# Spreading 1/rms over the partitions with the identity, and giving out the square-sum products later

## The chip, the core and the metric

The kernel runs on one core of a Trainium2 chip. Its five engines work side by side, each on its own queue: TensorE (PE in the profile, with its weight loads as PEld), VectorE (DVE), ScalarE (ACT), GpSimd (POOL) and SyncE (SP). The metric is the device time of one execution in microseconds (us); lower is better.

## The reference, cut to what matters

Two decoder layers run over 2048 prompt tokens and 8 sample tokens, 1024 channels wide. Every stage starts with a norm over the channels of a token:

```
def rms_norm(x, g):
    y = x * rsqrt(mean(x * x, axis=-1) + EPS)
    return y * g
...
x = x + mixer(rms_norm(x, norm_mix[l]))             # l = 0: conv branch (layer norm) and DeltaNet, l = 1: pooling
x = x + cross_attention(rms_norm(x, norm_xattn[l]))
...
y = rms_norm(x, norm_final)
```

The layer norm of the conv branch subtracts the mean over 512 channels first and divides by the root of the mean square in the same way.

## The kernel before, in words

Activations lie with channels on the 128 partitions and tokens along the free axis, so a sum over channels is a product on PE. All large products run as three products of a high and a low part (`mm3_steps`). The stages, by their times in the profile:

- `phase1`, to about 1137 us: the memory keys and values, then the input projection over five tiles of tokens (`DT`: three of 512, two of 260). The task `squares` (line 731) sums squares, the task `norms` (line 751) multiplies the roots in, and `dense_start` (line 791) gives PE its main work. The DeltaNet scan overlaps its end.
- `e2`, about 1137 to 1390 us: eight groups of 256 tokens (the first has 264, with the sample's 8). `norm` (line 1537) makes the layer norm of the conv branch.
- `attn` for layer 0, to about 1780 us, and again for layer 1, from about 2440 us to the end. `prep` (line 1640) makes the per-token roots, which go into the softmax's scale; `final` (line 1764) makes the last norm of layer 1.
- `odd_u` (line 1806), to about 2010 us, and `odd_g` (line 1958), to about 2440 us: the pooling mixer. Both multiply spread roots into what leaves PE; `odd_g` takes the roots that `odd_u` has stored in `rr`.
- `sample_attn` (line 2257) runs beside `attn` and `odd_g`: it streams keys and values through three buffers (`a_big`) and multiplies and sums them on DVE.

A norm has three steps. `square_sum` (line 1485) squares on ACT and adds on POOL into `w_sqa`. `token_rstd` (line 423) multiplies `w_sqa` by 64 columns of ones into `ps_ss`, one product per 128 tokens, so that each token's sum stands on its partition; twelve small DVE instructions make the root `rstd` (`rsqrt`, line 410). `spread` (line 437) brings the roots back along the free axis, the same on all partitions: DVE multiplies the identity by each column of roots into a diagonal matrix (`dg`, or the tile `w_sqq` by way of `tok_spread`, line 1512), and PE multiplies that by ones into `ps_bc`, one product over all tokens of the group. There are 37 such calls: 5 in `norms`, 8 each in `e2`, `odd_u`, `odd_g` and `final`. An f32 product is recorded as two passes, each with a weight load of 128 columns.

The order of each engine's queue is fixed when the program is written, by a planner (`Flow`). It keeps a clock for each engine with costs of its own. The main products are a generator; after each few of them `pump` (line 342) looks through the side tasks (`norms`, `prep` and so on). A task gives out instructions up to its next `yield`; `F.cur` is then the planner's time at which its last result is seen, and the task goes on when the planner's clock of PE has reached that (`_step`, line 332, puts `cur` into `item[1]`). A task that yields without having given out anything goes on at once. So a product of a norm stands in PE's queue where the planner believed its operand to be ready; if the operand is later than that, PE waits, since it takes its products in this order.

Of the kernel before, what the change touches and what calls it, by code (L numbers as in the profile page):

```python
# [7 lines left out]
F32 = mybir.dt.float32  # L8
# [397 lines left out]
NMORE = 2  # L406
XGAP, XSTART = 1000.0, 8


def rsqrt(F, pool, y, x, n, tag, eng="dve"):  # L410

# [22 lines left out]
    return r  # L434


def spread(F, C, pool, ppool, r, n, tag, dg=None):

    ncn = (n + 127) // 128
    if dg is None:  # L440
        dg = pool.tile([128, ncn * 128], F32, tag=tag + "dg", name="dg")
    for c in range(ncn):
        F.ts(dg[:, c * 128:(c + 1) * 128], C.ident, r[:, c:c + 1], ALU.mult)
    yield
    ps = getattr(ppool, "bgp", ppool).tile([128, 512], F32, tag="bg", name="ps_bc")
    F.mm(ps[:, 0:n], C.ones, dg[:, 0:n])
    return ps


def ceil128(n):  # L450
    return (n + 127) // 128 * 128
# [200 lines left out]
def phase1(F, C, I, D, st, P, R, mmp, bgp, loaders, mix, hp):  # L652
# [38 lines left out]
    with F.tile_pool(name="x1", bufs=1, side="right") as xp:  # L691
# [59 lines left out]
        def norms():  # L751
            for t, (o, n) in enumerate(DT):
                yield lambda: t in sums and (t < 4 or "kv" in sums)
                dg = xp.tile([128, 512], F32, tag="dg", name="dg", bufs=1)
                bc = yield from spread(F, C, xp, bgp, sums[t], n, "n", dg)
                for k in range(8):
                    x, _ = xs.pop((t, k))
                    F.stt(x, x, C.g_mix[:, 0, k:k + 1], bc[:, 0:n], ALU.mult, ALU.mult)
                    if k == 7:
                        F.now()  # L760
                    yield
                    F.copy(hs(t, 0, k), x)
                    yield
                    F.tt(hs(t, 1, k), x, hs(t, 0, k).bitcast(F32), ALU.subtract, eng=F.ve(n))
                    hfree.give()
                yield
                hdone.add(t)
# [742 lines left out]


def tok_spread(F, C, W, r, n):
    return spread(F, C, W.p, W, r, n, "w", dg=W.t("sqq", [128, ceil128(n)]))


def mm3(F, R, W, name, j, x, n):
# [4 lines left out]
    yield from mm3_steps(F, ps[:, 0:n], 8, (lambda k: w[0][:, k, :], lambda k: w[1][:, k, :]),  # L1521
                         (lambda k: x[0][:, k, :], lambda k: x[1][:, k, :]))
    return ps


SLACK = 1000


def e2(F, C, W, I, D, st, R, bdone, over, grow, spawn):

    ready = {}
    cv, sv = (x.rearrange("b p t -> p b t") for x in (D.c, D.sg))
    xv = I["xT"].rearrange("(k p) t -> p k t", p=128)

    ln, used = {}, set()

    def norm():

        for g in range(NG):
            n = gn(g)  # L1540
            yield lambda: g < 2 or g - 2 in used
            c = W.t("cd"[g % 2], [128, 4, n])
            load_cols(F, c, cv, g)
            yield
            cs = W.t("sqa", [128, n])
            F.red(cs, kt(c), ALU.add)
            yield
            ps = W.bgp.tile([128, 512], F32, tag="bg", name="ps_mean")
            F.mm(ps[:, 0:n], C.ones, cs)
            F.stt(c, ps[:, 0:n].unsqueeze(1).to_broadcast([128, 4, n]), -1.0 / 512, c, ALU.mult, ALU.add)  # L1550
            yield
            acc = square_sum(F, W, c, n)
            yield
            r = tok_rstd(F, C, W, acc, n, 1.0 / 512)
            yield
            ps = yield from tok_spread(F, C, W, r, n)
            F.tt(c, c, ps[:, 0:n].unsqueeze(1).to_broadcast([128, 4, n]), ALU.mult)
            yield
            for q in range(4):
                F.act(c[:, q, :], c[:, q, :], AF.Silu, scale=C.lng[:, q:q + 1], bias=C.lnb[:, q:q + 1])  # L1560
            ln[g] = c

    def prep():
        for g in range(NG):
            n = gn(g)
            sg = W.t("f", [128, 4, n])
            load_cols(F, sg, sv, g)
            yield lambda: g in ln
            c = ln.pop(g)
            F.tt(c, c, sg, ALU.mult)  # L1570
            yield lambda: bdone >= {2 * g, 2 * g + 1}
            b = W.t("f", [128, 4, n])
            F.dma(b, D.b[g])
            tb = F.cur
            F.now()
            res = W.xbuf if g % 2 == 0 else W.mbuf
            yield lambda: W.p2 is not None and res.ok()
            res.take()
            m = W.pair("x" if g % 2 == 0 else "m", n)
            yield from split_steps(F, m[0][:, 0:4], m[1][:, 0:4], c)  # L1580
            used.add(g)
            yield lambda: F.t["pe"] >= tb
            yield from split_steps(F, m[0][:, 4:8], m[1][:, 4:8], b)
            ready[g] = m, res

    def load_x(g, h):
        xr = W.t(f"y{h}", [128, 4, gn(g)])
        load_cols(F, xr, xv[:, 4 * h:4 * h + 4], g)
        return xr

    def dense():
        xr = {(0, h): load_x(0, h) for h in range(2)}
        grown = False

        def wait(cond):
            nonlocal grown
            yield from F.until(lambda: cond() or not grown and over())
            if not grown and over():
                grow()
                grown = True  # L1600
                yield from F.until(cond)

        for g in range(NG):
            n = gn(g)
            yield from wait(lambda: g in ready)
            m, res = ready.pop(g)
            for j in range(8):
                yield from wait(lambda: R.has("wo_e", j))
                ps = yield from mm3(F, R, W, "wo_e", j, m, n)
                if j == 7:  # L1610
                    res.give()
                h, q = j // 4, j % 4
                x = xr[g, h]
                F.tt(x[:, q, :], ps[:, 0:n], x[:, q, :], ALU.add)
                if q == 3:
                    F.dma(D.x1[g][:, 4 * h:4 * h + 4, :], x)
                    if g == 0:
                        F.copy(st.xs[:, 4 * h:4 * h + 4, :], x[:, :, 256:264])
                    if g + 1 < NG:
                        xr[g + 1, h] = load_x(g + 1, h)  # L1620
                if g == NG - 1:
                    R.free("wo_e", j)
                F.now()
            st.done.add(("x", 0, g))
            if g == 0:
                yield from wait(lambda: grown)
                spawn()

    F.spawn(norm(), 1)
    return prep(), dense()  # L1630


def attn(F, C, W, D, st, R, l, xin, xout):
# [6 lines left out]
    def prep():  # L1640
        for g in range(NG):
            acc, ch = None, []
            yield lambda: ("x", l, g) in st.done
            for h in range(2):
                x = W.t("f", [128, 4, 256])
                F.dma(x, xin[g][:, 4 * h:4 * h + 4, 0:256])
                yield
                if h == 0:
                    res = W.xbuf if g == 0 else W.mbuf
                    yield res.ok  # L1650
                    res.take()
                    xs = W.pair("x" if g == 0 else "m", 256)
                    yield W.sq.ok
                    W.sq.take()
                acc = square_sum(F, W, x, 256, acc, h == 1)
                yield from split_steps(F, xs[0][:, 4 * h:4 * h + 4], xs[1][:, 4 * h:4 * h + 4], x)
            yield
            r = tok_rstd(F, C, W, acc, 256, 1.0 / 1024)
            W.sq.give()
            r16 = W.t("r16", [128, 2], 2)  # L1660
            F.ts(r16, r, 1.0 / 16, ALU.mult)
            ready[g] = xs, r16
# [101 lines left out]
    def final(g, y):  # L1764
        yield W.sq.ok
        W.sq.take()
        acc = None
        for h in range(2):
            acc = square_sum(F, W, y[h], 256, acc, h == 1, "pool" if g < NG - 1 else "dve")
        yield  # L1770
        r = tok_rstd(F, C, W, acc, 256, 1.0 / 1024)
        yield
        ps = yield from tok_spread(F, C, W, r, 256)
        W.sq.give()
        for j in range(8):
            h, q = j // 4, j % 4
            F.stt(y[h][:, q, :], y[h][:, q, :], C.g_fin[:, j:j + 1], ps[:, 0:256], ALU.mult, ALU.mult)
            if q % 2:
                F.dma(D.o_y[g][:, j - 1:j + 1], y[h][:, q - 1:q + 1, :])
        if g + 2 < NG:  # L1780
            ys[g + 1] = load_y(g + 1)
        ydone.add(g)
# [23 lines left out]
def odd_u(F, C, W, I, D, st, R, rr):  # L1806
# [5 lines left out]
    def prep():  # L1812
        for g in range(NG):
# [4 lines left out]
            for h in range(2):  # L1818
# [7 lines left out]
                    xs = W.pair("x" if g % 2 == 0 else "m", n)  # L1826
                yield from split_steps(F, xs[0][:, 4 * h:4 * h + 4], xs[1][:, 4 * h:4 * h + 4], x)
            ready[g] = xs, res
            yield
            r = tok_rstd(F, C, W, acc, n, 1.0 / 1024)  # L1830
            F.vcopy(rr[:, g, 0:r.shape[1]], r)
            yield
            ps = yield from tok_spread(F, C, W, r, n)
            if g == 0:
                W.rb = W.t("rb", [128, 2, 264])
# [834 lines left out]
```

## Time and profile before

| | us |
|---|---|
| median of three runs (2884.25 to 2889.04) | 2886.37 |
| the profiled execution | 2889.38 |
| its span, first to last instruction | 2887.7 |
| PE busy (94% of the span), 20202 products | 2721.9 |
| PEld busy (86%) | 2494.4 |
| DVE busy (67%) | 1948.4 |
| ACT busy (35%) | 1012.6 |
| POOL busy (22%) | 647.4 |

Busy times are added per engine; engines overlap. What stands in brackets behind an instruction is the engine's idle time just before it and what ended that. A group "x8" is eight instructions in a row, with its first start and the time to its last end; the ends of products on PE are modelled, so distances between starts are the safer measure.

### The profile page before, as it was taken

What the parts mean: (1) busy time and instruction counts of PE and PEld (TensorE: products, weight loads), DVE (VectorE), ACT (ScalarE), POOL (GpSimd) and SP (SyncE); (2) the same over time, 40 slices, a digit from 0 to 9 for tenths busy, and PEclk for the clock granted to TensorE, in tenths of its full rate; (3) what the DMA queues carried; (4) which work ended last, traced back from release to release, by engine and by line L of the source; (5) the groups of instructions that cost most, each with busy time, mean ns of one, the idle gap of its engine ahead of it and who ended that gap; (6) DMA issues with size and microseconds to landing.
All of it is one profiled execution on the core that took longest, in us unless ns stands there. A gap on an engine that the chain in (4) does not pass through costs nothing.

```text
span 2887.7 us, 52194 instructions
## 1 busy us (share of the span) xinstructions
PE 2721.9 (94%) x20202; PEld 2494.4 (86%) x20202; DVE 1948.4 (67%) x4438; ACT 1012.6 (35%) x2388; POOL 647.4 (22%) x928
## 2 busy tenths in 40 slices
PE   7999999999999888799999999899999998999998
PEld 6878888888888777699888989899999998788987
DVE  6838999989678787776755556867655446665453
ACT  5632133233266454432322235444421113332321
POOL 3301112111053544123222320111012112221210
PEclk9999999999999998899999999899999999999999
DMA  7611122223355666565645434321535556421111
GB/s 240 213 50 41 45 71 56 61 74 115 118 148 160 200 205 189 184 214 190 205 154 165 151 106 145 105 74 67 185 129 169 178 169 201 135 76 67 67 60 51
DMA packets 260297, 377.85 MB, mean 131 GB/s; under 512 B 47440, under 2 KB 155728, under 8 KB 260048
## 3 DMA queue, kind: packets, MB, share of 16 engines
q1 hardware_dynamic: 181328, 267.13, 29.3%
q0 software_dynamic: 20864, 67.39, 7.5%
q10 hardware_dynamic: 57856, 39.99, 4.4%
q8 instruction: 159, 2.61, 0.4%
q14 instruction: 90, 0.74, 0.1%
HBM read 276.38 MB, written 96.40 MB: 129 GB/s over the span
## 4 chain that ended last, share of the span: by engine, by line
PE 51%; DVE 22%; DMA 11%; issue 4%; ACT 3%; POOL 1%; SPq 1%; DVEq 0%; ACTq 0%; POOLq 0%
PE ps_mm L168 44%; DVE cacc L225 7%; PE ps_bg L168 4%; DVE qacc L225 3%; DMA a_big<-d_sq 2%; DMA rraw<-d_VW 1%; DVE a_big L225 1%; DMA w_f<-d_x 1%; DMA a_big<-d_sp 1%; DVE rlo L219 1%; PE ps_pt L172 1%; PE ps_row L168 1%; DMA rraw<-d_G 1%; PE ps_bg L172 1%; POOL w_sqb L219 1%
## 5 line engine op out<-in xcount | busy, mean ns | idle before, releaser
L225 DVE SCALAR_TENSOR_TENSOR cacc<-glu,dww,cacc 128x1024 f32<-128x1024 f32 x240 | 325.0, 1367 | 5.9 <-ACT cacc L186 1.4
L219 POOL TENSOR_TENSOR rlo<-rraw,rhi 128x512 fp32r<-128x512 f32 x132 | 197.3, 1505 | 552.8 <-ACT rhi L186 487.0
L219 POOL TENSOR_TENSOR w_sqb<-w_sqb,w_sqq 128x512 f32<-128x512 f32 (+1 forms) x101 | 136.9, 1356 | 681.1 <-ACT w_sqq L186 668.6
L168 PE MATMUL ps_mm<-xh,rhi 128*128 128x256 f32 (+1 forms) x1920 | 272.2, 284 | 1.7 <-DVE w_y L219 1.7
L168 PE MATMUL ps_mm<-xl,rhi 128*128 128x256 f32 (+1 forms) x1920 | 272.9, 283 | 0.0
L168 PE MATMUL ps_mm<-xh,rlo 128*128 128x256 f32 (+1 forms) x1920 | 272.2, 283 | 0.0
L168 PEld LDWEIGHTS ps_mm<-xh,rhi 128*128 128x128 f32 x1920 | 248.9, 191 | 4.4 <-issue 2.1
L168 PEld LDWEIGHTS ps_mm<-xl,rhi 128*128 128x128 f32 x1920 | 249.2, 191 | 3.0
L168 PEld LDWEIGHTS ps_mm<-xh,rlo 128*128 128x128 f32 x1920 | 248.2, 191 | 0.9
L168 PE MATMUL ps_mm<-hh,rhi 128*128 128x512 f32 (+2 forms) x1152 | 217.9, 331 | 18.9 <-ACT hh L186 15.7
L168 PE MATMUL ps_mm<-hh,rlo 128*128 128x512 f32 (+2 forms) x1152 | 214.7, 328 | 0.0
L168 PEld LDWEIGHTS ps_mm<-hh,rhi 128*128 128x128 f32 x1152 | 179.0, 193 | 40.7 <-ACT hh L186 16.2
L168 PE MATMUL ps_mm<-hl,rhi 128*128 128x512 f32 (+2 forms) x1152 | 214.1, 328 | 0.0
L219 DVE TENSOR_TENSOR w_y<-ps_mm,w_y 128x256 f32<-128x256 f32 (+1 forms) x248 | 103.4, 420 | 161.8 <-PE ps_mm L168 157.8
L186 ACT ACTIVATE rhi<-rraw 128x512 fp32r<-128x512 f32 x224 | 137.4, 630 | 176.6 <-DMA rraw<-d_G 43.0
L168 PEld LDWEIGHTS ps_mm<-hh,rlo 128*128 128x128 f32 x1152 | 176.0, 190 | 19.8 <-issue 2.5
L225 DVE SCALAR_TENSOR_TENSOR a_big<-a_big 128x256 f32<-128x256 f32 x256 | 104.8, 448 | 130.8 <-DMA a_big<-d_sp 64.8
L168 PEld LDWEIGHTS ps_mm<-hl,rhi 128*128 128x128 f32 x1152 | 177.3, 192 | 17.3
L168 PE MATMUL ps_mm<-mh,rhi 128*128 128x256 f32 (+1 forms) x1152 | 169.7, 289 | 9.1 <-ACT mh L186 9.1
L168 PE MATMUL ps_mm<-ml,rhi 128*128 128x256 f32 (+1 forms) x1152 | 171.2, 290 | 3.3 <-DVE ml L219 3.3
L168 PE MATMUL ps_mm<-mh,rlo 128*128 128x256 f32 (+1 forms) x1152 | 165.6, 285 | 0.0
L168 PEld LDWEIGHTS ps_mm<-mh,rhi 128*128 128x128 f32 x1152 | 153.7, 196 | 11.3 <-ACT mh L186 9.8
(424 smaller groups left out, 5296.5 us busy)
## 6 DMA issues: line engine op xcount, KB each, us to landing
w_f<-d_x SPq DMA_DIRECT2D x60, 512.0 KB
d_x<-w_y SPq DMA_DIRECT2D x44, 512.0 KB
w_y<-d_x SPq DMA_DIRECT2D x44, 512.0 KB
a_big<-in_cache_k POOLq DMA_DIRECT2D x64, 256.0 KB, 4.3
a_big<-in_cache_v POOLq DMA_DIRECT2D x64, 256.0 KB, 4.2
rraw<-in_w_in SPq DMA_DIRECT2D x56, 256.0 KB
d_qkv<-so ACTq DMA_DIRECT2D x48, 256.0 KB
rraw<-in_w_xk SPq DMA_DIRECT2D x32, 256.0 KB
```

The lines of the kernel that those rows point to most:

```text
L168: self.nc.tensor.matmul(out, lhsT, rhs, start=start, stop=stop)
L172: self.nc.tensor.transpose(out, in_, ident)
L186: self.nc.scalar.activation(out=out, in_=in_, func=func, scale=scale, **kw)
L219: self._e(eng).tensor_tensor(out=out, in0=a, in1=b, op=op)
L225: self._e(eng).scalar_tensor_tensor(out=out, in0=a, scalar=s, in1=b, op0=op0, op1=op1, **kw)
```

## The change

The diagonal matrix goes. `spread` now makes one product per 128 tokens: the column of roots, repeated 128 times by its access pattern, is the one operand, and the identity the other, and each goes into its own columns of `ps_bc`. With it go the tiles for the diagonal and the `yield` that stood between it and the product; the callers lose one `yield` too, as `spread` begins with one. And a constant `LAG_S` of 2000 (ns of the planner's clock) is added to `F.cur` ahead of the products that sum squares (and, in `e2`, that sum the values) for all groups but the first: the planner gives them out 2 us later. `squares` and `norms` of `phase1`, `odd_g` and `final` get no such lag.

```diff
+LAG_S = 2000.0
...
-def spread(F, C, pool, ppool, r, n, tag, dg=None):
-    ncn = (n + 127) // 128
-    if dg is None:
-        dg = pool.tile([128, ncn * 128], F32, tag=tag + "dg", name="dg")
-    for c in range(ncn):
-        F.ts(dg[:, c * 128:(c + 1) * 128], C.ident, r[:, c:c + 1], ALU.mult)
+def spread(F, C, pool, ppool, r, n):
     yield
     ps = getattr(ppool, "bgp", ppool).tile([128, 512], F32, tag="bg", name="ps_bc")
-    F.mm(ps[:, 0:n], C.ones, dg[:, 0:n])
+    for c in range((n + 127) // 128):
+        m = min(128, n - 128 * c)
+        F.mm(ps[:, c * 128:c * 128 + m], r[:, c:c + 1].to_broadcast([128, 128]), C.ident[:, 0:m])
     return ps
...
         def norms():
                 yield lambda: t in sums and (t < 4 or "kv" in sums)
-                dg = xp.tile([128, 512], F32, tag="dg", name="dg", bufs=1)
-                bc = yield from spread(F, C, xp, bgp, sums[t], n, "n", dg)
+                bc = yield from spread(F, C, xp, bgp, sums[t], n)
...
 def tok_spread(F, C, W, r, n):
-    return spread(F, C, W.p, W, r, n, "w", dg=W.t("sqq", [128, ceil128(n)]))
+    return spread(F, C, W.p, W, r, n)
...
-SLACK = 1000
@@ e2, norm
             F.red(cs, kt(c), ALU.add)
+            F.cur += LAG_S if g > 0 else 0.0
             yield
             ps = W.bgp.tile([128, 512], F32, tag="bg", name="ps_mean")
...
             acc = square_sum(F, W, c, n)
+            F.cur += LAG_S if g > 0 else 0.0
             yield
             r = tok_rstd(F, C, W, acc, n, 1.0 / 512)
-            yield
             ps = yield from tok_spread(F, C, W, r, n)
@@ attn, prep
+            F.cur += LAG_S if g > 0 else 0.0
             yield
             r = tok_rstd(F, C, W, acc, 256, 1.0 / 1024)
@@ attn, final
         r = tok_rstd(F, C, W, acc, 256, 1.0 / 1024)
-        yield
         ps = yield from tok_spread(F, C, W, r, 256)
@@ odd_u, prep
             ready[g] = xs, res
+            F.cur += LAG_S if g > 0 else 0.0
             yield
             r = tok_rstd(F, C, W, acc, n, 1.0 / 1024)
             F.vcopy(rr[:, g, 0:r.shape[1]], r)
-            yield
             ps = yield from tok_spread(F, C, W, r, n)
```

## Rows read from the trace of the kernel before

**Rows 1.** Busy time of each engine in the last stretch, 2560 to 2888 us.

```profile
core 0: us, PE busy (x) PEld busy (x) DVE busy (x) ACT busy (x) POOL busy (x), PEclk, DMA share, GB/s
2560.00:2888.00 328.00, 313.32 (x2091) 286.17 (x2089) 151.43 (x466) 84.20 (x183) 53.85 (x47) 0.98 0.18 63
```

**Rows 2.** Whom PE waited for, whole span: us in total, times, longest us.

```profile
PE ps_bc L168 <- DVE w_sqq L232: 15.3, 5, 3.4
PE ps_ss L168 <- POOL w_sqa L219: 13.7, 9, 5.9
PE ps_mean L168 <- DVE w_sqa L246: 11.4, 2, 11.0
```

**Rows 3.** Timeline of PE: a product with repeated column and identity; one with a diagonal.

```profile
777.71 1.05 PE L168 MATMUL ps_bg<-ident,gc 128*128 128x128 f32 x8
778.59 0.60 PE L172 MATMUL ps_bg<-ident,k 128*128 128x128 f32 x4
...
2076.29 0.59 PE L168 MATMUL ps_bc<-w_sqq,ones 128*128 128x256 f32 x2
2076.53 1.08 PE L168 MATMUL ps_mm<-mh,rhi 128*128 128x264 f32 x6
```

**Rows 4.** Costliest groups, DVE: the multiplications that make the diagonals (largest of three).

```profile
L232 DVE TENSOR_SCALAR w_sqq<-ident,rstd 128x128 f32<-128x128 f32 x50 | 11.8, 279 | 0.1
```

**Rows 5.** Timeline of the first two tiles in phase 1, from square-sum to spread.

```profile
34.11 0.72 PE L168 MATMUL ps_mm<-hh,rhi 128*128 128x256 f32 x4
...
40.54 0.16 DVE L225 SCALAR_TENSOR_TENSOR rstd<-rt,rstd 128x4 f32<-128x4 f32 x1
40.73 0.88 DVE L232 TENSOR_SCALAR dg<-ident,rstd 128x128 f32<-128x128 f32 x4
...
41.66 1.22 PE L168 MATMUL ps_bc<-dg,ones 128*128 128x512 f32 x1 [3.06 <-DVE dg L232]
...
67.77 0.72 PE L168 MATMUL ps_mm<-hh,rlo 128*128 128x256 f32 x4
...
72.43 0.16 DVE L225 SCALAR_TENSOR_TENSOR rstd<-rt,rstd 128x4 f32<-128x4 f32 x1
...
77.15 0.86 DVE L232 TENSOR_SCALAR dg<-ident,rstd 128x128 f32<-128x128 f32 x4
...
78.06 1.12 PE L168 MATMUL ps_bc<-dg,ones 128*128 128x512 f32 x2 [1.06 <-DVE dg L232]
...
78.62 0.68 PE L168 MATMUL ps_mm<-hh,rhi 128*128 128x256 f32 x1
```

**Rows 6.** Timeline around one wait of PE in odd_g, all engines.

```profile
2225.27 0.43 DVE L225 SCALAR_TENSOR_TENSOR a_big<-a_big 128x256 f32<-128x256 f32 x1 [3.77 <-DMA a_big<-d_sq]
...
2225.96 0.76 DVE L219 TENSOR_TENSOR ml<-w_d,mh 128x256 fp32r<-128x256 f32 x2
...
2227.16 0.47 DVE L232 TENSOR_SCALAR w_sqq<-ident,rr 128x128 f32<-128x128 f32 x2
...
2227.78 0.67 PE L168 MATMUL ps_bc<-w_sqq,ones 128*128 128x256 f32 x2 [3.42 <-DVE w_sqq L232]
...
2228.10 3.89 PE L168 MATMUL ps_mm<-ml,rhi 128*128 128x256 f32 x18
```

**Rows 7.** Busy time in two stretches, before and after that wait; columns as in rows 1.

```profile
2212.00:2224.00 12.00, 12.00 (x103) 12.00 (x102) 5.41 (x21) 2.94 (x8) 2.67 (x5) 1.00 0.49 149
2228.70:2232.10 3.40, 3.40 (x18) 3.40 (x18) 1.76 (x3) 0.42 (x1) 0.99 (x2) 0.50 0.57 140
```

**Rows 8.** Whom PE waited for from 1137 to 1790 us, the square-sums.

```profile
PE ps_ss L168 <- POOL w_sqa L219: 3.9, 7, 0.9
```

**Rows 9.** Timeline at the long waits for square-sums and sums: e2, then odd_u.

```profile
1179.00 0.68 DVE L219 TENSOR_TENSOR o<-o,of 128x512 f32<-128x512 f32 x1
1179.14 1.22 PE L168 MATMUL ps_mean<-w_sqa,ones 128*128 128x256 f32 x2 [11.01 <-DVE w_sqa L246]
...
1829.55 1.52 DVE L219 TENSOR_TENSOR ml<-w_f,mh 128x1024 fp32r<-128x1024 f32 x1
...
1830.04 1.11 PE L168 MATMUL ps_ss<-ones,w_sqa 128*128 128x64 f32 x4 [5.89 <-POOL w_sqa L219]
...
1852.19 0.66 PE L168 MATMUL ps_ss<-ones,w_sqa 128*128 128x64 f32 x4 [3.91 <-POOL w_sqa L219]
```

## The prediction, made before the changed kernel was run

> **What bounds the kernel now.** I began with the page's busy shares and then took the stretches one by one. PE is the engine that the time hangs on: in the last stretch it is busy 313 of 328 us while DVE is busy for 151 [rows 1], and over the span it leaves about 166 of 2888 us. So an added product costs its full length, and what can be saved is PE's waiting. The view of who waited for whom says how much of that belongs to the norms [rows 2]: 15.3 us for the diagonal matrix, 13.7 us for the square-sums, 11.4 us for the sums of `e2`. A wait is worth less than its length, though, if what stands next in PE's queue is late too, so I looked at the timeline behind the long ones. And a wait has an echo: after one of 3.42 us PE ran at the lower of its two levels (granted clock 0.50, 1.2 GHz) and got 18 products through in 3.4 us, where 103 in 12 us are its pace at 1.00 (2.4 GHz) [rows 7]. That is 0.19 against 0.117 us each, 1.3 us lost per such stretch. What PE had done before the fall was to stand idle for 3.42 us.
>
> **The products (+7.9 us).** A product with a repeated column and the identity already stands in the trace: four of 128 columns make eight passes, and the next instruction starts 0.88 us after the first, 0.11 per pass. A 256-wide product with the diagonal takes 0.24 us for its two [rows 3]. The change turns two passes into four: 0.44 against 0.24, +0.20 each for 29 calls (seven groups each in `e2`, `odd_u`, `odd_g`, eight in `final`), 5.8 us. The three groups of 264 take six passes, 0.66 for 0.24, +1.3 us in all. In phase 1 three tiles of 512 take eight passes, 0.88 against the 0.56 us from 78.06 to 78.62 [rows 5], +1.0, and two of 260 go as the 264 do, +0.8. Together +8.9. I take 1.0 off for the calls that will run while PE waits anyway (four in `odd_g`, one at the end). Bounds: 0, if all fell into waits, to 8.9.
>
> The Trainium skill speaks to this in "TensorE: Matmul & The Clock Gate". Its section "Back-to-back issue gap" gives an isolated product N/2.4 + 2.5 ns, so 56 ns for 128 columns, and by that four passes would take 223 ns, this term would be about zero and the forecast 7.9 us lower, near 2871. Its section "LDWEIGHTS (loading the stationary operand)" makes a load cost 1/1.2 ns per column whatever else it does, 107 ns for 128, so that splitting a product is paid for per piece. Rows 3, with 0.11 us per pass, side with the second and leave the first no chance.
>
> **The diagonals on DVE (0).** 85 multiplications leave DVE, 279 ns each in the largest group [rows 4], at most 24 us in all. I count nothing: DVE has room beside PE in every stretch that PE fills [rows 1]. Where the cover fails, in `odd_g` and at the end, it is counted below. Bounds: 0 and a gain of those 24 us, if DVE's queue made PE's waits everywhere; I take the lower, as the waits shown have other causes.
>
> **odd_g (-6.4, and -2.6 of the clock).** Four of the eight spreads here hold PE, 12.3 of the 15.3 us. In the timeline of one [rows 6] PE waits 3.42 us for the diagonal, but the diagonal waits in DVE's queue behind a multiplication for the sample's attention, which waits for its DMA until 2225.27. The changed product needs only roots that have been in `rr` for long, so PE passes it. Next in its queue stands a product that reads `ml`, and that stands in the same DVE queue, at 2225.96, done some 0.4 us later. PE could go on at about 2226.5 instead of 2228.10: 1.6 us, not 3.4. I take this four times, 6.4. Bounds: 0, if the sample's DMA holds `ml` longer, and 12.3. What is left of each wait is near 2 us; waits of 1 us in rows 5 are not what rows 7 shows, so I let two of the four slow stretches go, 2 x 1.3. Bounds 0 and 5.2.
>
> **The lag (-7.3).** Moving a product back by 2 us of the planner's clock puts some 17 others ahead of it. In `e2` and `attn` 0 the seven waits for square-sums are 0.9 us at most, 3.9 together [rows 8], shorter than the lag: I take 3.5. The 11.01 us of `e2` I count at 0.6: the next work behind it needs `o`, which DVE makes only at 1179.00 to 1179.68 [rows 9], so PE would stand there instead. In `odd_u` the wait of 5.89 us gives 1.0: next comes a product on the same group whose `ml` is there only at 1831.07, 1 us after PE went on [rows 9]. The one of 3.91 us stands in the middle of the group before, whose operands are all there; the lag takes its 2.0 off, and perhaps the echo; I give that 0.2. Sum 3.5 + 0.6 + 1.0 + 2.2 = 7.3. Bounds: 0, and the 19 us that rows 8 and 9 make without the wait of `e2` for `o` and with their echoes. What the lag holds up: the roots come 2 us later, to the softmax's scale in `attn`, to the spread in `odd_u` and to the layer norm in `e2`. Each is made one group ahead, over 20 us before its use, except for the second group of a stage, where PE has nothing else to do and the lag of the planner's clock costs no time on the chip. Nothing new waits on DVE, POOL or SP; no DMA is moved.
>
> **Phase 1 (+1.4).** `norms` is a task of its own, without a lag. Before, it gave out the diagonal and then waited for the planner to see it, and other products went ahead. Now its `yield` comes first, with nothing given out, so the product follows at once when `sums[t]` is set, and that happens when the root's instructions are given out, not when they are done. For the first tile `norms` is waiting: the diagonal came right behind the root (40.54, 40.73). So PE would stand from 34.11 to the root's end at 40.70, 6.6 us, where it stood for 3.06 [rows 5]: +3.5. For the second tile the diagonal came at 77.15, 4.6 us after the root: `norms` was still busy with the first, and the new product will find its root done. That takes away the wait of 1.06 there, and I take the third tile to go like the second: -2.1. Bounds: -5 to what the second rival costs.
>
> **The end (-0.6).** The last spread has no cover: two multiplications leave, 0.28 us each [rows 4].
>
> **Sum.** 7.9 + 0 - 6.4 - 2.6 - 7.3 + 1.4 - 0.6 = -7.6 us against the profiled execution's 2889.4 (span 2887.7 and 1.7 around it): 2881.8. The median of the runs is 3.0 lower, at 2886.4, so I forecast 2878.8 for it. About 0.2%, 5.8 us, is what a measurement of this kernel can tell from no change.
>
> **Rivals.**
>
> *The waits only change their names (chance 0.22).* PE passes the spread and waits at once for `ml` as long as before, since the sample's DMA rules DVE's queue. For it: the DVE row of rows 6 shows 3.77 us of idle time for that DMA. Against: once it lands, `ml` comes before the diagonal. `odd_g` then gives nothing: -7.6 + 9.0 = +1.4, 2888.
>
> *The product is given out too early in phase 1 (0.16), the one that ends slower.* If `norms` is waiting for its sums at every tile, PE stands from the square-sum to the end of the root five times. For the second tile that is 67.77 to 72.59, 4.8 us [rows 5]; four times that in place of the -2.1 and of nothing makes 21 us on top of the forecast: 13 slower, about 2900; if only one more tile does it, or the waits are 2 to 3 us as a bare root would take, some 2889 to 2893. It decides when the previous tile's work ends before the next sums are given out; the 4.6 us between root and diagonal speak against it for the second tile, and nothing shown speaks for the others.
>
> *The lag does nothing (0.10).* It moves places in a queue by the planner's clock. If that clock already runs behind the chip where the waits are, the products land in the same places. Then -7.6 + 7.3: -0.3, 2886.
>
> *More goes than I count (0.17).* The order of all later work is dealt anew. If the four slow stretches all go (2.6 more), the waits of `odd_g` shrink by 3.4 instead of 1.6 (7 more) and the echo of 3.91 us goes, the sum is -18: 2868.
>
> **Chances.** The forecast has 0.35, over 2874 to 2884, of which 0.25 lie beyond 0.2%. Faster by over 0.2% (under 2880.6): that 0.25, the fourth rival's 0.17, 0.06 of the first and 0.02 of the third, with a lucky order of the rest: 0.50. Slower (over 2892.1): 0.12 of the second, 0.05 of the first: 0.17. Within: 0.33. The range goes from 2864, a little beyond the fourth rival, to 2893, where the milder form of the second lies; that leaves out 0.11 of the second, 0.05 of the fourth and 0.03 of the first.
>
> **What would show it.** Right: in `odd_g` PE's waits for DVE at `ps_bc` are gone and waits at `ps_mm<-ml` of 1 to 2 us stand there; `ps_bc` shows four passes 0.11 us apart; waits at `ps_ss` below 1 us from 1137 to 1790 us are gone; one wait of 6 us at `ps_bc` near 35 us and none at the other tiles. Wrong: waits for the root at several tiles of phase 1; the same total wait in `odd_g` under other names; new waits on rows that I count as covered, DVE's above all; or a time outside the range with these steps as forecast, which would mean that the new order of the rest decides.

## The result, and the profile after

The changed kernel takes 2904.13 us (median of five runs, 2901.6 to 2914.6) against 2886.3 us of the kernel before in the same sessions: a ratio of 1.0080, 95% interval 1.0064 to 1.0096. It is slower by 18 us by the medians and 23 by the ratio, where the forecast was 8 us faster and the range ended at 2893. The profiled execution has a span of 2912.8 us at a mean granted clock of 0.971 (before: 2887.7 and 0.972), so a lower mean clock does not explain the loss.

The page's first part, then the last stretch as in [rows 1], shifted by 26 us:

```profile
PE 2733.0 (94%) x20298; PEld 2507.8 (86%) x20298; DVE 1938.3 (67%) x4346; ACT 1013.6 (35%) x2391; POOL 655.7 (23%) x935
```

```profile
2586.00:2914.00 328.00, 312.79 (x2101) 286.99 (x2099) 146.61 (x443) 85.10 (x183) 54.29 (x47) 0.98 0.19 63
```

There are exactly 96 more products, and DVE is 10 us less busy. The last stretch looks as before. The loss is in the middle. I took the start of the first product of each stage in both timelines (for `e2` the first product into `ps_mean`, so that the end of the scan lies within it) and compared how long the stages last. By these starts `odd_u` begins at 1812 us before, `odd_g` at 2057 and `attn` of layer 1 at 2465, later than the rounded times given for the stages. After against before: phase 1 up to the scan +1.6 us, scan +4.3, `e2` +8.3, `attn` of layer 0 +10.4, `odd_u` -2.1, `odd_g` +2.8, `attn` of layer 1 -0.2. Nineteen of 25 us lie in `e2` and `attn` 0, where I had expected a gain of 4.

Whom PE waited for, whole span (answers to [rows 2]), and then from 1137 to 1837 us (answers to [rows 8]):

```profile
PE ps_bc L168 <- DVE rstd L225: 18.9, 9, 5.4
PE ps_mm L168 <- DVE ml L219: 17.4, 8, 4.5
PE ps_pt L172 <- DVE xl L219: 10.8, 6, 3.2
PE ps_ss L168 <- POOL w_sqa L219: 6.8, 4, 2.3
```

```profile
PE ps_pt L172 <- DVE xl L219: 8.5, 5, 3.2
PE ps_bc L168 <- DVE rstd L225: 6.7, 5, 3.0
PE ps_ss L168 <- POOL w_sqa L219: 4.2, 2, 2.1
```

The waits for the diagonal are gone and those for the square-sums are halved, and waits for the bare root, for `ml` and for `xl` (3.3 and 7.6 us before) stand there instead.

The new product in PE's timeline (answers to the second half of [rows 3]):

```profile
2098.59 0.61 PE L168 MATMUL ps_bc<-ident,rr 128*128 128x128 f32 x4
2098.95 1.69 PE L168 MATMUL ps_mm<-mh,rhi 128*128 128x264 f32 x12
```

Four passes hold PE for 0.36 us, from the start of the first to the start of the next product; two with a diagonal took 0.24.

The first tile of phase 1 (answers to the first part of [rows 5]):

```profile
33.01 1.10 PE L168 MATMUL ps_ss<-ones,acc 128*128 128x64 f32 x8 [0.43 <-DVE acc L219]
...
39.28 0.16 DVE L225 SCALAR_TENSOR_TENSOR rstd<-rt,rstd 128x4 f32<-128x4 f32 x1
39.50 2.08 PE L168 MATMUL ps_bc<-ident,rstd 128*128 128x128 f32 x8 [5.39 <-DVE rstd L225]
```

PE stands for 5.39 us behind the square-sum until the root is there, and at no other tile of phase 1.

A wait in `odd_g` (answers to [rows 6]), all engines, and the granted clock in two stretches behind it (answers to [rows 7]):

```profile
2249.79 0.42 DVE L225 SCALAR_TENSOR_TENSOR a_big<-a_big 128x256 f32<-128x256 f32 x1
...
2250.14 0.76 DVE L219 TENSOR_TENSOR ml<-w_d,mh 128x256 fp32r<-128x256 f32 x2
...
2250.95 2.62 PE L168 MATMUL ps_mm<-ml,rhi 128*128 128x256 f32 x13 [1.98 <-DVE ml L219]
...
2258.15 0.38 PE L168 MATMUL ps_mm<-ml,rhi 128*128 128x256 f32 x1 [1.39 <-DVE ml L219]
```

```profile
2251.00:2253.30 2.30, 2.30 (x13) 2.30 (x14) 2.30 (x7) 0.42 (x1) 0.62 (x3) 0.63 0.35 114
2258.40:2262.00 3.60, 3.60 (x32) 3.60 (x32) 2.04 (x4) 1.06 (x1) 0.19 (x1) 1.00 0.47 179
```

PE has passed the spread and stands at `ml`, which waits in DVE's queue behind the sample's multiplication, the picture of the first rival. A new wait in `e2`, the stage of the first rows of [rows 9], DVE and PE:

```profile
1216.51 0.69 DVE L219 TENSOR_TENSOR rlo<-rraw,rhi 128x512 fp32r<-128x512 f32 x1 [2.32 <-ACT rhi L186]
1217.12 0.15 DVE L234 TENSOR_SCALAR ms<-ps_ss 128x2 f32<-128x2 f32 x1
...
1219.28 0.16 DVE L225 SCALAR_TENSOR_TENSOR rstd<-rt,rstd 128x2 f32<-128x2 f32 x1
...
1219.59 0.68 PE L168 MATMUL ps_bc<-ident,rstd 128*128 128x128 f32 x4 [2.96 <-DVE rstd L225]
```

The root starts late, since DVE stands 2.32 us for the split of a weight ahead of it, and PE waits at the new product for the root's last instruction. Before, PE had no wait at this group's spread.

Over the main products of `e2` and the start of `attn` 0, from 1200 to 1420 us, this is whom PE waited for, before and then after:

```profile
PE ps_ss L168 <- POOL w_sqa L219: 1.6, 3, 0.7
PE ps_cs L168 <- DVE a_s L246: 1.0, 1, 1.0
PE ps_mean L168 <- DVE w_sqa L246: 0.4, 1, 0.4
```

```profile
PE ps_bc L168 <- DVE rstd L225: 5.9, 4, 3.0
PE ps_row L168 <- POOL a_big L219: 2.6, 4, 1.0
PE ps_row L168 <- ACT a_rb L186: 2.2, 3, 1.3
PE ps_row L168 <- DVE a_big L219: 1.0, 3, 0.4
PE ps_mm L168 <- DVE ml L219: 0.2, 1, 0.2
```

Of the 3.0 us of before, 1.0 was at a product of the sample's attention (`ps_cs`). Of the 11.9 us after, 5.9 are at the spread of the root and 5.8 at the sample's products (`ps_row`); at the operands of a group's main products PE waits for 0.2 us.

### The profile page after: what moved, and what is told of

The parts are those of the page before. It is cut to its first block, busy times and chain, and to the rows that moved or that the text cites. A ratio compares the mean times of both kernels' runs of the same rounds, so it can differ in the third digit from the quotient of the medians.

```text
span 2912.8 us, 52307 instructions
## 1 busy us (share of the span) xinstructions
PE 2733.0 (94%) x20298; PEld 2507.8 (86%) x20298; DVE 1938.3 (67%) x4346; ACT 1013.6 (35%) x2391; POOL 655.7 (23%) x935
## 4 chain that ended last, share of the span: by engine, by line
PE 42%; DMA 14%; DVE 12%; issue 4%; ACT 3%; POOL 1%; SPq 1%; DVEq 0%; ACTq 0%; POOLq 0%
PE ps_mm L168 35%; PE ps_bg L168 3%; DMA a_big<-d_sp 3%; DMA a_big<-d_sq 2%; DVE a_big L225 2%; DVE rlo L219 1%; DMA w_f<-d_x 1%; DMA a_big<-in_cache_v 1%; PE ps_pt L172 1%; DMA a_big<-in_w_xq_n 1%; PE ps_row L168 1%; PE ps_bg L172 1%; DVE w_d L219 1%; DMA rraw<-d_VW 1%; POOL w_sqb L219 1%
## 5 line engine op out<-in xcount | busy, mean ns | idle before, releaser
L219 POOL TENSOR_TENSOR rlo<-rraw,rhi 128x512 fp32r<-128x512 f32 x139 | 207.9, 1506 | 546.2 <-ACT rhi L186 444.2
L168 PEld LDWEIGHTS ps_mm<-ml,rhi 128*128 128x128 f32 x1152 | 153.0, 194 | 20.3 <-DVE ml L219 19.3
```

The costliest lines, as they stand in the source:

```text
L168: self.nc.tensor.matmul(out, lhsT, rhs, start=start, stop=stop)
L219: self._e(eng).tensor_tensor(out=out, in0=a, in1=b, op=op)
```

## The experiments

The kernel before was run beside each group; its medians were 2882.0, 2883.8, 2876.6, 2880.0 and 2881.6 us. Single runs of one kernel lie up to 18 us from its median, so one profile tells where time goes better than how much; the ratios tell how much.

### One part of the change at a time

**The product in pieces, diagonal kept.** The rest of the order is as before.

```diff
-    F.mm(ps[:, 0:n], C.ones, dg[:, 0:n])
+    F.pe_op(max(n, 64) * 1.69, ps[:, 0:n], C.ones, dg[:, 0:n])
+    for c in range(ncn):
+        s = slice(c * 128, min(n, c * 128 + 128))
+        F.nc.tensor.matmul(ps[:, s], C.ones, dg[:, s], start=True, stop=True)
```

> The kernel before with its diagonal kept and every instruction in the place it had; only the product with the diagonal is cut into one product per 128 tokens. If added passes on PE are paid at their length, 96 more of them cost 8 to 9 us over the kernel before (ratio 1.003). If the passes fall into waits, nothing (1.000). If PE pays more for them than the rows of before say, over 12 us. Were the changed kernel's 18 to 25 us all due to the passes, this run would show them.

Measured: 2884.71 us, ratio 1.0002 (0.9984 to 1.0021). By the interval the added passes cost 6 us at most. A call of four passes holds PE for 0.36 us here too.

**The new product in the old order.** DVE's multiplications go, the planner goes on to count them, so nothing else moves.

```diff
-        F.ts(dg[:, c * 128:(c + 1) * 128], C.ident, r[:, c:c + 1], ALU.mult)
+        F._op("dve", 130 + 128 / 1.92, [dg[:, c * 128:(c + 1) * 128]], [C.ident, r[:, c:c + 1]])
...
+        F.nc.tensor.matmul(ps[:, c * 128:c * 128 + m], r[:, c:c + 1].to_broadcast([128, 128]), C.ident[:, 0:m], start=True, stop=True)
```

> The changed product (repeated roots by the identity, no diagonal on DVE) but every other instruction in the order of the kernel before: the planner is still told of the diagonal and of one product. If freeing PE from the diagonal is worth what I counted in odd_g (6 to 9 us) the two cancel: within 3 us of before. If the waits only change their names there, 6 to 9 us slower, as the run with the split product. If the changed kernel's loss lies in the form of the product, 18 us or more.

Measured: 2883.43 us, 0.9999 (0.9985 to 1.0014). Within some 4 us, the reach of the interval, the new product by itself neither costs nor gives. In `odd_g` of this profile the waits only change their names: PE waits nowhere at `ps_bc`, where the kernel with the product in pieces waits 9.8 us, and 12.6 us for `ml`, where that one waits 3.3.

**The change without its lag** (`LAG_S = 0.0`).

> The changed kernel with a lag of 0. If the loss comes from products of the roots that are given out too early (PE waits for rstd, 19 us in the changed kernel), it stays: 15 to 20 us over before. If the lag makes it, this is within 5 us of before plus passes, under 10 us over.

Measured: 2884.34 us, 1.0013 (0.9997 to 1.0029). The new product in its new places costs 8 us at most. Stage by stage the profile of the change is longer than this one by 11.6 us in `e2`, 4.1 in `attn` 0 and 5.3 to 5.7 in each later stage (in sum more than the medians differ, as the change's profile is of its longest run). So of the 10.4 us that `attn` 0 is longer than before, 6.3 are there without the lag, and `e2` is the one stage that stands out in either comparison.

**The lag alone, on the kernel before** (`F.cur += LAG_S if g > 0 else 0.0` at the same four places, diagonal kept).

> The kernel before with the lag of 2 us alone, diagonal and its yields kept. If the lag takes PE's waits at the square-sums away, 3 to 8 us faster than before. If it costs by holding the roots up, or by dealing the order of the sample's work anew, slower by 5 to 15 us. If it does nothing on the chip, within 3 us.

Measured: 2905.15 us, 1.0083 (1.0066 to 1.0101). The lag makes the whole loss. It does do what it was forecast to do; whom PE waited for in this kernel, whole span:

```profile
PE ps_bc L168 <- DVE w_sqq L232: 23.4, 11, 4.7
PE ps_bg L172 <- DVE o L219: 17.5, 4, 11.1
PE ps_pt L172 <- DVE xl L219: 11.8, 5, 4.2
...
PE ps_cs L168 <- DVE a_s L246: 3.4, 1, 3.4
...
PE ps_ss L168 <- POOL w_sqa L219: 1.5, 1, 1.5
...
PE ps_mean L168 <- DVE w_sqa L246: 0.8, 1, 0.8
```

The square-sums fall from 13.7 to 1.5 us and the sums from 11.4 to 0.8. But the 11 us stand at `o` now, as forecast, and the spread, the softmax (`xl`) and the sample's products take up the rest and more.

### Which place

**The lag in `e2` only, in `attn` only, in `odd_u` only**, each on the kernel before:

> The kernel before, with the lag of 2 us only in e2 (ahead of the sums and of the square-sums). The lag at all four places cost 23 us (2905.2 against 2882.0). Theory A, the loss starts in e2: there the roots come late for the spread, PE waits for them, and the sample's multiplications are dealt anew; the profile of the lag at all places loses 11 of its 15 us in e2. Then this kernel is 11 to 20 us slower than before, 2893 to 2902. Theory B, any new order costs as much, wherever it starts: 2890 to 2905 here and about the same for each of the three kernels of one place. Theory C, the loss lies in attn and odd_g: this kernel within 4 us of before.

> The kernel before, with the lag of 2 us only in prep of attn. Theory A: the order of e2 stays, and what is lost is the few us that attn shows with all four lags: 2883 to 2888. Theory B: 2890 to 2905. Theory C: 2890 to 2900.

> The kernel before, with the lag of 2 us only in prep of odd_u. Theory A: no loss or a gain of up to 2 us, 2880 to 2884, since the wait of 3.91 us for a square-sum falls and the dense work covers the rest. Theory B: 2890 to 2905. Theory C: 2885 to 2892, through the order in odd_g.

Measured: `e2` 2894.42 us, 1.0045 (1.0020 to 1.0070); `attn` 2888.01, 1.0025 (1.0008 to 1.0042); `odd_u` 2882.76, 1.0000 (0.9985 to 1.0016). The three sum to 1.0070, near the 1.0083 of all. `e2` carries most, `attn` a part, `odd_u` nothing, neither loss nor the 3.2 us of gain that I had counted there: in its profile the 9.8 us of waits for square-sums are gone from that stage, and 4.4 us at the spread and 4.2 us at `mh` stand there instead.

With the lag in `attn` only, the profile has longer waits at the softmax of `attn` 0. Whom PE waited for from 1390 to 1820 us with the lag in `attn`, and what DVE waited for there, first with the lag, then before:

```profile
PE ps_pt L172 <- DVE xl L219: 8.7, 4, 3.7
...
PE ps_pt L172 <- DVE w_mns L242: 2.0, 1, 2.0
```

```profile
DVE a_big L225 <- DMA a_big<-d_sp: 43.8, 15, 5.1
```

```profile
DVE a_big L225 <- DMA a_big<-d_sp: 26.1, 13, 3.7
```

The same stretch of before has 4.5 us at `ps_pt<-xl`. The two longest of these waits, 3.7 and 3.0 us, follow a multiplication of the sample that stood ahead of `xl` in DVE's queue and waited for its DMA. But DVE's added 17.7 us cannot be put down to the lag. In the profiles of the two runs that kept the order of before (the product in pieces, and the new product in the old order), which take the time of before, the same row is 41.3 and 40.9 us, and the wait at `xl` 6.9 us in both. So the profile leaves some 2 us at the softmax to the lag; that it costs in `attn` at all is shown by the time (1.0025), not by these rows.

### How it costs

**A lag of 0.5 us at all four places**:

> The kernel before, with a lag of 0.5 us in place of 2 us at all four places. If the loss goes with the length of the lag (roots late by so much), a quarter of it is left: 2885 to 2889. If it comes from dealing the later work anew, whatever the lag, 2890 to 2910, with no relation to the length.

Measured: 2896.16 us, 1.0045 (1.0026 to 1.0064), runs from 2878 to 2905. A quarter of the lag leaves half of the loss, so it does not shrink in proportion.

**4 us instead of 2 in `e2`**:

> The kernel before with a lag of 4 us in place of 2 in e2 alone (2 us there gave 2894.4, 12.9 or a ratio of 1.0045 more). Theory B, the chain: the normed values of a group are finished 6 us ahead of their use with 2 us, some 10 us with none; twice 2 us more per group takes most of the rest, and each of six groups then waits 1 to 3 us more, with echoes: 2905 to 2925. Theory A, new places: no relation to the length, 2880 to 2900.

Measured: 2913.04 us, 1.0114 (1.0080 to 1.0147), two and a half times the loss of 2 us. In the main part of `e2` the profile has 18.3 us of PE's waits at the sample's products and 13.0 at main products. Among the latter are plain waits for the group's own operand at groups 1, 5, 6 and 7, of 1.3 to 3.7 us; the first (timeline, ACT and PE):

```profile
1213.92 1.04 ACT L186 ACTIVATE mh<-w_f 128x1024 fp32r<-128x1024 f32 x1
...
1215.02 1.22 PE L168 MATMUL ps_mm<-mh,rhi 128*128 128x256 f32 x4 [2.83 <-ACT mh L186]
```

That led to a number that I should have read before: the **reserve**, the time from the end of ACT's split of the second half of a group's operand (`xh` or `mh` from `w_f`, made by the same task behind the normed first half) to the first product of that group. In the timeline of before, for group 2:

```profile
1236.12 1.04 ACT L186 ACTIVATE xh<-w_f 128x1024 fp32r<-128x1024 f32 x1
...
1240.91 1.07 PE L168 MATMUL ps_mm<-xh,rhi 128*128 128x256 f32 x8
```

3.7 us. So for groups 1 to 7, in us (the second half is needed at the fifth product, so a small negative number is not yet all a wait):

| kernel | 1 | 2 | 3 | 4 | 5 | 6 | 7 | length of `e2` against before |
|---|---|---|---|---|---|---|---|---|
| before | 10.9 | 3.7 | 1.4 | 10.4 | 13.7 | 14.4 | 15.0 | |
| lag 2 us in `e2` | 1.2 | -1.7 | 8.2 | 11.8 | 10.2 | 13.2 | 10.6 | +12.4 |
| lag 4 us in `e2` | -4.2 | -2.3 | 2.3 | -0.7 | -1.8 | -2.5 | -0.8 | +35.0 |
| change without lag | 9.0 | 12.1 | 13.1 | 14.4 | 17.7 | 21.4 | 21.1 | -3.2 |
| the change | 5.0 | 5.5 | 2.9 | 5.3 | 11.3 | 14.4 | 10.2 | +8.3 |

A longer lag takes more of the reserve, and with 4 us PE stands at operands. But the reserve is not what the change pays with: its thinnest, 2.9 us, is not under the thinnest of before, 1.4, PE waits 0.2 us at operands there, and `e2` is longer all the same. With 2 us in `e2` on the kernel before, the one wait at an operand is 0.9 us (group 2), where the waits at the sample's products in the main part of `e2` make 8.5 us (before: 1.0).

**The lag in groups 1 to 3 of `e2`** (the diff), **or in groups 4 to 7** (`g > 3` in its place):

```diff
-            F.cur += LAG_S if g > 0 else 0.0
+            F.cur += LAG_S if 0 < g < 4 else 0.0
```

> The kernel before with the lag of 2 us in e2 for its groups 1 to 3 alone. In the trace of before, the last part of a group's operand is finished 10.9, 3.7 and 1.4 us ahead of the group's first product for these groups, and 10.4 to 15.0 us ahead for groups 4 to 7. Theory B, the chain of the norm eats this reserve of up to two lags per group: the whole loss of e2 is here, 2888 to 2896. Theory A, new places: it could stand in either half, 2876 to 2896 with no preference.

> The kernel before with the lag of 2 us in e2 for its groups 4 to 7 alone, whose operands are finished 10.4 to 15.0 us ahead of their use. Theory B: no loss, 2876 to 2885. Theory A: as the other half, 2876 to 2896 with no preference.

Measured: first groups 2898.32 us, 1.0060 (1.0038 to 1.0083); last four 2889.97, 1.0037 (1.0024 to 1.0050). The first half seems to cost more, though the intervals overlap. The second is not free, as theory B had it, and both together (1.0045) cost less than the two added up. With the lag in the last four, the reserves of groups 4 to 7 fall to 2.2, 2.6, 1.4 and 1.9 us, and none is used up. `e2` gets 5.8 us longer, and the next stage, which has no lag in this kernel, 8.0. The timeline at the start of `attn` 0, ACT and PE:

```profile
1419.88 0.60 PE L172 MATMUL ps_pt<-ident,w_c 128*128 128x128 f32 x4
...
1424.12 0.63 ACT L186 ACTIVATE w_sqq<-w_f 128x512 f32<-128x512 f32 x1 [1.97 <-DMA w_f<-d_x]
1426.12 0.63 ACT L186 ACTIVATE w_sqq<-w_f 128x512 f32<-128x512 f32 x1 [1.37 <-POOL w_sqb L219]
1426.65 1.04 ACT L186 ACTIVATE mh<-w_f 128x1024 fp32r<-128x1024 f32 x1
1427.60 0.58 ACT L186 ACTIVATE xh<-ps_pt 128x512 fp32r<-128x512 f32 x1
...
1428.96 1.12 PE L172 MATMUL ps_pt<-ident,w_c 128*128 128x128 f32 x4 [8.48 <-DVE xl L219]
```

The stages' preparing tasks run one behind the other. With `e2` late, the squares of group 1 of `attn` stand in ACT's queue ahead of the softmax's copy `xh<-ps_pt`, one of them waiting for its DMA; PE stands for 8.48 us. Before, the last of these squares started at 1411.51, ahead of the first transposes at 1416.86, and the copy followed within 0.1 us.

**Without the sample's attention**, without and with the lag at all four places:

```diff
 def sample_attn(F, C, W, I, D, st, l):
+    if l == 0:
+        F.dma(D.x2[0][:, :, 256:264], st.xs, eng=E)
+        st.done.add("s0")
+        return
+    F.dma(D.o_y_s, st.xs, eng=E)
+    st.done.add("s1")
+    return
```

> The kernel before without the attention of the 8 sample tokens in both layers (its products, its multiplications on DVE and its loads are left out; the sample's values pass it unchanged). It is the base for the next run. Estimate from the waits: PE's waits for the sample's rows and for what stands in DVE's queue behind its multiplications make some 20 to 40 us with their echoes, the products themselves about 10: 2830 to 2865.

> The same without the sample's attention, with the lag of 2 us at all four places. Theory A, the lag costs through the sample's attention: its products and multiplications are dealt into other places of the queues of PE, DVE and ACT, where their data or their DMA is late, and what stands behind them waits. Then with that attention left out the lag costs nothing, this kernel within 6 us of the last one. Theory B, the lag costs through the norms themselves (in e2 the chain from the sum to the normed values grows by two lags per group, and in attn the scale of the softmax comes later): then about 20 us slower than the last one, as with the sample's attention.

Measured: 2784.14 us, 0.9672 (0.9642 to 0.9701), far below my estimate: the sample's attention costs 92 us, not the 30 to 50 of waits and products that I had added up. With the lag 2794.68, 0.9714 (0.9686 to 0.9742). The medians differ by 10.5 us, and each of the four runs with the lag is slower than each of the four without. (The two intervals overlap, but both carry the spread of the kernel before.) So without the sample's attention the lag still costs about half of its 23 us: more than theory A's 6, less than theory B's 20. In the profiles `e2` (+0.2) and `attn` 0 (-0.9) lose nothing to the lag now; the 6 us by which these differ come from `odd_u` (+3.8) and `attn` of layer 1 (+5.2), less small gains elsewhere. And `e2` loses nothing although its reserves at groups 1 and 2 are -3.1 and -0.6 us and PE waits 3.9 us at operands there. So a used-up reserve alone made no loss in `e2`, and its loss comes with the sample's steps in the queues. What costs in the later stages, with the sample gone, was not followed up. With the lag in `e2`, sample present, PE's timeline at the start of group 2 shows the two side by side:

```profile
1235.35 0.74 PE L168 MATMUL ps_mm<-xh,rhi 128*128 128x256 f32 x4 [0.94 <-ACT xh L186]
...
1237.92 0.60 PE L168 MATMUL ps_row<-a_big,a_hx 128*8 128x512 f32 x1 [1.60 <-DVE a_big L219]
```

### On the changed kernel

**The lag left in `odd_u` alone; taken out of `e2`; taken out of `attn`:**

> The changed kernel with the lag taken out of e2 and attn, left in odd_u alone. If the places add up as they did on the kernel before (12.9 for e2, 7 for attn, 0 for odd_u), it is as fast as before within 6 us: 2876 to 2888. If the loss of the changed kernel comes from the lag in odd_u together with the new product, it stays at 2895 to 2905.

> The changed kernel with the lag taken out of e2, left in attn and odd_u. If the places add up: 5 to 8 us slower than before, 2883 to 2893. If with the new product, which is given out without a yield behind the root, the lag in e2 is free (the trace of the changed kernel shows its operands 2.9 to 14.4 us ahead) and the loss is all in attn: 2895 to 2905.

> The changed kernel with the lag taken out of attn, left in e2 and odd_u. With the lag in odd_u alone it stood at a ratio of 1.0009 to before, with attn and odd_u at 1.0024, with all at 1.008. If e2 carries most of the loss on the changed kernel too: 1.005 to 1.008, 2892 to 2904. If the two places only cost together (the reserve that e2 uses up is missed in attn, where the lag asks for more of it): 1.001 to 1.004, 2882 to 2892.

Measured: 2883.12 us, 1.0009 (0.9994 to 1.0024); 2889.30, 1.0024 (1.0011 to 1.0037); 2898.93, 1.0068 (1.0041 to 1.0094). Against 1.0080 for the whole change, the lag in `e2` costs 0.0056 or 16 us. That in `attn` costs 0.0012 or 3.5 us, which the intervals do not tell from nothing, and the rest 0.0009. With the lag out of `e2`, PE's waits from 1200 to 1420 us are 1.1 us at the spread and 0.4 at the sample's products, in place of 5.9 and 5.8.

**One lag more, ahead of the new product** (`F.cur += LAG_B` of 2000 before `spread`'s `yield`):

> The changed kernel (all its lags) with one lag more: the products that spread the roots are given out 2 us later on the planner's clock, in all five tasks that use them. In the changed kernel PE waits 18.9 us for roots at these products. Theory R, the reserve: a third lag in e2's chain makes the normed values later still, and the time goes up by 5 to 20 us, 2905 to 2925. Theory W, the price is in the waits for the root at the new product, which the planner gives out too early: they go, and the time comes down by 8 to 19 us, 2884 to 2897.

Measured: 2897.13 us, 1.0052 (1.0031 to 1.0072). That is the edge of what W foresaw, and not slower, against R. The waits for the root fall from 18.9 to 8.2 us, with none left in `e2`, and yet `e2` loses 2.5 us more against the change, its reserves at groups 1 and 2 at -1.4 and 1.6; `attn` 0 is 8.3 us shorter. So the waits for the root may be a part of the price (the intervals of this kernel and of the change overlap a little), but taking them away in `e2` did not make `e2` shorter. No version that does the whole work is faster than the kernel before.

## Why the prediction was wrong

**The step that failed** is the end of "The lag (-7.3)", which put what the lag holds up at nothing: "Each is made one group ahead, over 20 us before its use". Those 20 us are the way from a root to the main products of its group (21 to 31 us for groups 1 to 7 of `e2` before). But the first product that takes a root in `e2` is its spread. That started 1.3 to 2.8 us behind the end of the root before, with the diagonals between, and 0.1 to 0.3 us behind it in the changed kernel. There PE now waits 5.9 us, at four of the groups. The step also gave no cost to what the lag does to the places of other work: at the sample's products PE waits 5.8 us in place of 1.0. PE's idle time in the main part of `e2` goes from 6.6 to 13.2 us, and that part gets 8.1 us longer.

Shown by times: the lag alone makes the loss (1.0083), and the change without it does not (1.0013). Most of it comes with the lag in `e2`: taken out of the change there, 1.0080 becomes 1.0024. Shown by the profiles: with the lag out of `e2` both kinds of waits shrink there (1.1 and 0.4 us), and with 4 us of lag PE waits at the normed operands too. Not settled: how the time divides between the spread, the sample's products and the later stages. The run that took the waits at the spread out of `e2` made `e2` no shorter, and without the sample's attention `e2` lost nothing to the lag, but the kernel still some 10 us. That the two halves of `e2` cost more than the whole, and 0.5 us at all places as much as 2 us in `e2`, says that the new places of other work alone are worth several us.

**The gain of the lag** was sized on waits that do go (13.7 to 1.5 us with the lag alone), but PE then stands at the next thing. I had asked what is late next only for the two longest waits.

**The products** (+7.9) were mis-sized: +0.12 us for a 256-wide call, not +0.20. I had taken 0.11 per pass from a row of eight; four passes here go at 0.09. By the lengths in the changed kernel's trace (medians of 0.36, 0.59 and 0.81 us for four, six and eight passes) the term would be 5 to 6 us, an estimate, and the run of the product in pieces allows 6 us at most. The two figures that I took from the Trainium skill, "TensorE: Matmul & The Clock Gate", sections "Back-to-back issue gap" and "LDWEIGHTS (loading the stationary operand)", give 0.22 and 0.43 us for four passes; the trace, with 0.36, agrees with neither. The first section calls its formula one for an isolated product and gives about 81 ns for 128 columns in a stream of weight loads and products, which I passed over. By that figure four passes take 0.32 us, an estimate, and of the three it is the nearest to the trace.

**The diagonals** at 0: right as far as the runs can tell; without them and with the new product, in the old order, the time is the same (0.9999).

**`odd_g`** (-6.4 and -2.6): wrong; the first rival, "the waits only change their names", held here. The 12.3 us at `ps_bc` are gone, but `ps_mm<-ml` went from 3.3 to 17.2 us, and PE is idle for 25.3 us of the stage in place of 25.4. The four longest waits there are 4.5, 3.7, 2.9 and 2.0 us where I had put 2 each, and behind one of 1.98 us the granted clock did fall.

**Phase 1** (+1.4): right in place and near in size: 5.39 us at the first tile against 6.6, nothing at the others, the stage +1.6. So the second rival, the one on the slower side, was false, and the kernel is slower for a reason that none of the rivals had.

**The chances**: 0.17 for slower was drawn from phase 1 and `odd_g`; the lag had only bounds of "0, and the 19 us" of gain, no loss. Excluding a loss there needed a row for the product that takes the root next, and I gave none.

## What to carry to other kernels

When an instruction of a side chain is moved back, look at every product that takes its result, the nearest first: here the main products stood 21 to 31 us away, and the spread 1.3 to 2.8. Measure also how far ahead of its use the chain's last result is finished, group by group and across the seam to the next stage; a long delay draws on that too. A wait that goes away is worth only what the next instructions in the same queue let through. And in a program whose order is dealt by a planner, run each part of a change by itself with the order held fixed before giving the change its price: here the new product was free within the noise, and two microseconds in a planner's clock cost twenty. And before a row of a changed kernel's profile is put down to the change, look at the same row in a run that kept the order.

## What was unexpected of the hardware

- Cutting a 256-wide f32 product into two of 128 raises PE's hold from 0.24 to 0.36 us, but 37 such calls cannot be seen in the time (1.0002, 0.9984 to 1.0021).
- A wait of 1.98 us was followed by a stretch at a mean granted clock of 0.63, so partly at the lower of the two levels (1.2 GHz); one of 1.39 us, some 6 us later, was followed by 1.00 (2.4 GHz). Before the first PE had run a stream of products without a pause at 1.00; before the second it had run without a wait since the first, in part at the lower level.
- DVE's waits for the sample's DMA (`d_sp`) in `attn` 0 make 26.1 us in the profile of before, and 41.3 and 40.9 us in the two runs that kept its order, at the same time of the whole kernel (1.0002 and 0.9999).
